# Four small moves in a two-layer attention kernel: context sums, context rows, the first pair's transposes, the gate products

## The chip, the core and the metric

One core of a Trainium2 chip. The time is the device time of one launch, in microseconds (us); a kernel's time is the median of its runs. The engines are named as the profile names them: PE (TensorE) does matmuls and transposes, DVE (VectorE), ACT (ScalarE) and POOL (GpSimd) work on rows, and SP (SyncE) issues most of the DMAs. ACT can issue DMAs too; an issue stands in ACT's queue like any instruction.

## The reference

Two adaLN-modulated blocks over 1024 latent tokens with a prefix of 256 context tokens, model width 1024, all in fp32. Layer 0 has grouped-query attention (16 heads of 64, 4 key heads), layer 1 latent attention (16 heads; keys and values from a compressed width of 256 and a shared rotary key of 32). Cut to one block:

```python
shift, scale, gate = split(silu(c) @ w_mod + b_mod, 3)
h = rms_norm(x, norm_w) * (1 + scale) + shift        # context: hc, with c_ctx
q, k, v, g = projections of h (and of hc)            # norms, rotary
o = softmax(q k^T * s) v      # latent queries: context and latent keys; context queries: context keys alone
x = x + gate * ((o * silu(g)) @ w_out)               # layer 0 does it for the context too
```

The output is the latent stream after both layers.

## The kernel before

Matmuls run on fp32r operands that are split into a high and a low part, so that a product is three matmuls: high by high (L120), low weight (L121), low activation (L122). The order on each engine is that of the code wherever a `manual_schedule` stands around it.

The program runs in stages, in this order: modulation and layer 0's projections; layer 0's attention; layer 0's output projection, which also makes the normed, modulated and transposed input of layer 1; layer 1's kv stage (compress, norm, expand to keys and values, tile by tile, as a software pipeline of stages written with `staged`); its q stage and gates; layer 1's attention; its output projection.

*Attention* (`Attention.run`) goes over units: a unit is a head group's or head's queries with its list `kts` of key tiles of 128. In layer 0 there are 20 units, 16 for latent queries ("lat", ten key tiles) and four for context queries ("ctx", two key tiles), the latter at positions 4, 9, 18 and 19. Layer 1 has 16 units of ten key tiles. For each unit the PE makes scores `st`, ACT the exponentials `p` of a tile of 128 x 1024 (L607), and the PE multiplies them with the values (L654, `av` or `avt`). Beside the scores of one unit the PE makes the maxima `mx` of a unit further on, which DVE reduces to `m` (L454, L486, L495, L497); the reduced maxima are turned (`turn` in `do_shift`, L95) and the rows written by DMA (L521) as `shift` or `shift_ctx`, which later scores subtract. The denominators are made in two ways. POOL adds a unit's `p` tiles into `acp` (`add_up`, L640); what it has not added is summed by DVE in blocks of 32 x 32 (`squares`, L99; then `total_by_squares`: four turns L95, two sums L705 and L706, the reciprocal L707), or else the PE sums `acp` by a matmul with a constant (`twos`, L720, then L724 and L725 on DVE). `total` chooses between the two by whether the unit has `squares`. SP then stores the reciprocals (`rrow`), reads them back spread over rows (`rb`) beside the SiLU gates (`sg`), POOL multiplies (L739, L740) and SP stores the result (`od`). In `run`, `n1` is how many of a unit's tiles POOL adds; `late` marks a context unit among the last two.

*The first output projection* (`out_proj(0, ...)`) goes over ten token tiles: `oraw` is loaded, split into `oh` (ACT) and `ol` (DVE), 48 matmuls make `y`, and DVE and POOL add gate times `y` to the residual `xt`. Its `sink0` stores the row, normalizes it (`norm_rows`) and, at every second tile, calls `flush`, which runs `modulate` for a pair of tiles: 16 PE transposes (L319) from the normalized `xt` (L307), then `hmod` on DVE, `hh` on ACT, `hl`. `hold` keeps pairs that are complete; a tile's sink is run before the next tile's matmuls are issued, so that `flush` at tile index 2 puts the transposes of pair 0 (tiles 0 and 1) between the matmuls of tile index 2 and those of tile index 3, the fourth.

*Layer 1's gate* is the product of `u` (the row silu(c)) with the third part of the modulation weights. It is made on DVE: for each of eight blocks `wcols` (512 KB) one `mod_cols` (L265), and at the end `mod_cols_end(2)`, which adds the bias (L271), turns (L95) and stores the row as `gated` (L274). The row is read back as `gb` when layer 1's output projection begins. In the kernel before this stands in the kv stage: the pipeline's third stage, `later_with_cols`, fetches and multiplies one block in each of the first eight tiles. `wcols` takes its buffers from `rawp` (`wraw`), from which the weights and the first `oraw` come too.

Of the kernel before, what the change touches and what calls it, by code (L numbers as in the profile page):

```python
# [10 lines left out]
F32 = mybir.dt.float32  # L11
# [8 lines left out]
P = 128  # L20
D = 1024
KT = D // P
# [4 lines left out]
TT = NT // P  # L27
# [5 lines left out]
def raw(ap):  # L33
    return ap.bitcast(F32)
# [3 lines left out]
def hybrid_kernel(ctx: ExitStack, tc: tile.TileContext, ins: dict, out: bass.AP):  # L38
# [31 lines left out]
    ud = dram.tile([2, D], F32, name="ud")  # L70
# [55 lines left out]
    def staged(items, *stages):  # L126

        items = list(items)
        held = {}
        for t in range(len(items) + len(stages) - 1):  # L130
            for j, stage in enumerate(stages):
                i = t - j
                if 0 <= i < len(items):
                    held[i] = stage(items[i], held.get(i))
# [127 lines left out]
    def mod_cols(w, u, junk, sec, k, conds):  # L262

        for j in conds:
            dve.scalar_tensor_tensor(junk, w, 0.5, u[:, j, :], op0=ALU.mult, op1=ALU.mult, accum_out=sums_of[sec][:, k, j:j + 1])  # L265
# [94 lines left out]
    class Attention:  # L360
        def __init__(self, l, units, ops):
            self.l, self.units, self.ops = l, units, ops
            self.state = {}
            self.vcache = {}
            self.kcache = {}
            self.sm = sm_pool
            self.step = 0
            self.deferred = []
            self.totals = []
            self.sums = 0  # L370
            self.running = False
            self.turns = []
            self.started = 0
            self.done = 0
            self.todo = []
            self.last_lat = [u for u in units if u["kind"] == "lat"][-1]

        def open_early(self, st):
# [131 lines left out]
        def do_shift(self, u):  # L510

            s = self.state[id(u)]
            m = tops[self.units.index(u) % 4]
            dve.reduce_max(m[:, :8], s["m"], axis=AX.X)

            def turn():
                at_ = (0, 32, 96)[self.units.index(u) % 3]
                r = turned[at_:at_ + 32, :]
                turn_squares(r, raw(m))
                for n in range(2):  # L520
                    (act if self.running else sp).dma_start(raw(s["crow"][n]), r[4 * n:4 * n + 4, :])  # L521

            self.turns.append((self.units.index(u), turn))

# [227 lines left out]
        def run(self, lead, ahead, extra, tail):  # L752
# [4 lines left out]
            with tc.manual_schedule(engines={mybir.EngineType.PE, mybir.EngineType.DVE, mybir.EngineType.Activation, mybir.EngineType.Pool}):  # L757
                for t, u in enumerate(self.units):
# [20 lines left out]
                    for group in (kts[:cut], kts[cut:]):  # L779
                        if not group:  # L780
                            continue
                        end = group[-1] == kts[-1]
                        final = t == len(self.units) - 1 and end
                        p2s = [self.pp.tile([P, 2, 1024], F32, name="p", tag="p", bufs=5) for _ in range(len(group) // 2)]
                        ps = [p2[:, a, :] for p2 in p2s for a in range(2)]

                        late = not whole and t >= len(self.units) - 2
                        n1 = len(ps) - (4 if end and (cut or final) else 2 if late or (whole and end) else 0)
                        for i, kt in enumerate(group):
                            self.run_deferred(self.step)  # L790
                            if HALVES[self.l]:
                                count += 1 if WIDE[self.l] else 2
                                self.scores_by_halves(u, kt, ps[i], self.next_maxima(count, t + 1 + ahead))
                            else:
                                self.do_scores(u, kt, ps[i], one_more)
                            self.step += 1
                            if i < n1:
                                self.add_up(u, [ps[i]], [])
                        if end and t + 2 < self.started:
                            self.state[id(self.units[t + 2])].pop("rest", lambda: None)()  # L800
                        if final:
                            tail()
                        if WIDE[self.l] and group[0] == kts[0]:
                            self.av_tile(u)
                        self.run_turns(next_turn)
                        if final:
                            self.add_up(u, [], ps[n1:])
                        if final:
                            self.run_deferred(self.step + 2)
                        gap = 0  # L810
                        while self.totals and (whole or late or final):
                            self.totals.pop(0)(gap, True)
                            gap += 3
                        if end and (whole or late) and not final:
                            if late:
                                self.add_up(u, [], [])
                            self.squares(u, p2s[n1 // 2:])
                        if t % 2 and end:
                            if parts:
                                parts()  # L820
                            parts = extra.pop(0)() if extra else None
                        self.do_av(u, group, ps)
                        self.step += (2 + len(group)) // 3
# [776 lines left out]
    with ExitStack() as st:  # L1600
# [16 lines left out]
        def sink0(tt, xt):  # L1617
            if tt < TL:
                sp.dma_start(x1d[tt * P:(tt + 1) * P, :], xt)
            norm_rows(xt, small)  # L1620
            xs_of.setdefault(tt // 2, []).append(xt)
            if tt % 2 == 0:
                flush(1)
            else:
                hold.append((tt // 2, xs_of[tt // 2]))

        def started0():
# [33 lines left out]
    with ExitStack() as st:  # L1661
# [96 lines left out]

        kept = []

        u = st.enter_context(tc.tile_pool(name="urow1", bufs=1, **right)).tile([P, D], F32, name="u0", tag="u0")
        sp.dma_start(u, ud[0:1, :].broadcast_to([P, D]))

        def gate_cols(k):
            w = rawp.tile([P, D], F32, name="wcols", tag="wraw")
            sp.dma_start(w, ins["l1_w_mod_t"][2 * D + k * P:2 * D + (k + 1) * P, :])
            mod_cols(w, u.unsqueeze(1), w, 2, k, (0,))
            if k == KT - 1:
                mod_cols_end(2)

        def store_all_but_last(tt, held):
            kept.append(held) if tt == TT - 1 else kv_store(tt, held)

        def later_with_cols(tt, kv):
            if tt < KT:
                gate_cols(tt)
            return kv

        with in_order(mybir.EngineType.DVE):
            staged(range(TT), kv_compress, kv_latent, later_with_cols, later, kv_expand, store_all_but_last)  # L1780
        wqa = load_weight(w_in1, KT, 288, 384)
        with tc.manual_schedule(engines={mybir.EngineType.PE, mybir.EngineType.DVE}):
            early[0] = proj1(0, wqa, 384)
# [234 lines left out]
    stL, stLP = ExitStack(), ExitStack()  # L2018
    at.open_late(stL, stLP)
    first = []  # L2020
    at.run(24, 2, pieces, lambda: first.extend(fetch_first(1, 3)))
    stLP.close()
    stE.close()
# [54 lines left out]
```

## Time and profile before

| | us |
|---|---|
| median of three runs | 1639.27 (1636.88 to 1641.38) |
| the profiled execution | 1638.23 |
| its span in the trace | 1636.3 |
| PE busy | 1596.0 |
| DVE busy | 1150.5 |
| POOL busy | 961.7 |
| ACT busy | 641.2 |

The profiled execution's own time is 1.93 us over its span. A row of the trace has the start, the duration, the engine, the line of the kernel, the operation, the tiles (out<-in), their shapes and a count where equal rows follow each other; in square brackets stands for how long the engine was idle before and what ended that. A matmul's row lasts longer than the distance to the next one, since matmuls overlap. "PEclk" is the clock that was granted to the PE, as a share of full speed.

### The profile page before, as it was taken

To read this page: it belongs to the slowest core of one execution; us is meant where nothing else is said; L and a number is where in the kernel's file an instruction comes from. 1 tells how busy PE (TensorE), PEld (TensorE's weight loads), DVE (VectorE), ACT (ScalarE), POOL (GpSimd) and SP (SyncE) were. 2 spreads that over 40 slices of the span, in tenths; PEclk is the share of its full clock that TensorE was granted. 3 is DMA by queue.
4 is the path that set the end of the run, shared out by engine and by line. 5 is a ranking of instruction groups with operands and counts; after the bars stand their busy time and mean duration, and the time that the engine had idled before them with its cause. 6 is when DMAs were issued, how large, how long until landed. Compare 5 with 4: busy or idle time off the path is not lost.

```text
span 1636.3 us, 26486 instructions
## 1 busy us (share of the span) xinstructions
PE 1596.0 (98%) x9788; PEld 1178.3 (72%) x9788; DVE 1150.5 (70%) x1951; ACT 641.2 (39%) x943; POOL 961.7 (59%) x629
## 2 busy tenths in 40 slices
PE   7999999999999999999989999999999999999998
PEld 5776788865554555577878798987776767767587
DVE  2674876679998988746576767755778888788231
ACT  3652321235654555522244543341444544435310
POOL 2673640138999999923245555450768878777521
PEclk9999999999999999999999999999999999999999
DMA  8636566742533342274246867768456565562451
GB/s 285 213 106 192 170 196 231 215 134 56 130 82 98 94 108 78 71 224 152 96 138 182 239 200 201 221 202 197 114 137 154 124 149 117 136 145 70 131 179 64
DMA packets 215325, 246.77 MB, mean 151 GB/s; under 512 B 19802, under 2 KB 157266, under 8 KB 215196
## 3 DMA queue, kind: packets, MB, share of 16 engines
q1 hardware_dynamic: 214228, 244.83, 53.7%
q8 instruction: 77, 1.26, 0.3%
q14 instruction: 52, 0.43, 0.1%
q10 hardware_dynamic: 968, 0.25, 0.1%
HBM read 171.23 MB, written 73.63 MB: 150 GB/s over the span
## 4 chain that ended last, share of the span: by engine, by line
PE 84%; DMA 5%; DVE 4%; POOL 2%; ACT 2%; issue 2%; SPq 1%; DVEq 0%; POOLq 0%; ACTq 0%
PE st L600 21%; PE avt L654 9%; PE av L654 9%; PE mm L120 8%; PE mm L122 8%; PE mm L121 8%; PE mx L452 4%; PE y L120 3%; PE y L121 3%; PE y L122 3%; PE mx L486 2%; DVE wb L163 1%; DMA q1l<-tl 1%; PE mx L462 1%; DMA mraw<-in_l_w_mod 1%
## 5 line engine op out<-in xcount | busy, mean ns | idle before, releaser
L640 POOL TENSOR_TENSOR acp<-acp,p 128x1024 f32<-128x1024 f32 x188 | 448.6, 2386 | 12.6
L607 ACT ACTIVATE p<-st 128x1024 f32<-128x1024 f32 x328 | 336.3, 1027 | 154.5 <-PE st L600 145.7
L454 DVE TENSOR_REDUCE m<-mx 128x1 f32<-128x512 f32 x256 | 175.8, 691 | 66.2 <-PE mx L452 60.3
L640 POOL TENSOR_TENSOR acp<-p 128x1024 f32<-128x1024 f32 x34 | 81.5, 2398 | 191.7 <-ACT p L607 191.7
L495 DVE TENSOR_REDUCE m<-mx 128x1 f32<-128x1024 f32 x128 | 150.2, 1219 | 39.4 <-PE mx L486 38.9
L654 PE MATMUL avt<-p,v 128*64 128x512 f32 x672 | 149.3, 596 | 0.7 <-ACT p L607 0.6
L654 PE MATMUL av<-p,v 128*64 128x512 f32 x640 | 141.1, 595 | 0.0
L163 POOL TENSOR_TENSOR wb<-wraw,wa 128x512 fp32r<-128x512 f32 (+3 forms) x65 | 91.0, 1415 | 80.4 <-ACT wa L184 80.4
L120 PE MATMUL mm<-wa,hh 128*128 128x512 f32 (+2 forms) x336 | 126.1, 375 | 1.7 <-ACT hh L1041 1.1
L600 PE MATMUL st<-QH,KH 64*128 64x512 f32 x320 | 122.5, 407 | 0.6 <-DVE gth L354 0.5
L122 PE MATMUL mm<-wa,hl 128*128 128x512 f32 (+2 forms) x336 | 121.5, 362 | 1.6 <-DVE hl L1044 1.6
L121 PE MATMUL mm<-wb,hh 128*128 128x512 f32 (+2 forms) x336 | 121.1, 360 | 0.0
L600 PE MATMUL st<-QH,KL 64*128 64x512 f32 x320 | 117.9, 391 | 0.0
L600 PE MATMUL st<-QL,KH 64*128 64x512 f32 x320 | 117.6, 390 | 0.0
L654 PEld LDWEIGHTS avt<-p,v 128*64 128x64 f32 x672 | 46.0, 137 | 93.8 <-issue 82.9
L654 PEld LDWEIGHTS av<-p,v 128*64 128x64 f32 x640 | 44.3, 137 | 87.9 <-issue 87.3
L120 PE MATMUL mm<-hh,wa 128*128 128x512 f32 (+1 forms) x264 | 103.0, 390 | 0.9 <-ACT th L102 0.9
L120 PE MATMUL y<-wa,oh 128*128 128x512 f32 (+1 forms) x268 | 103.3, 386 | 0.0
L122 PE MATMUL y<-wa,ol 128*128 128x512 f32 (+1 forms) x268 | 102.8, 384 | 0.0
L121 PE MATMUL y<-wb,oh 128*128 128x512 f32 (+1 forms) x268 | 102.8, 384 | 0.0
L122 PE MATMUL mm<-hh,wb 128*128 128x512 f32 (+1 forms) x264 | 101.3, 384 | 0.0
L121 PE MATMUL mm<-hl,wa 128*128 128x512 f32 (+1 forms) x264 | 101.3, 384 | 0.0
(267 smaller groups left out, 4045.1 us busy)
## 6 DMA issues: line engine op xcount, KB each, us to landing
wraw<-in_l_w_in SPq DMA_DIRECT2D x28, 512.0 KB
wcols<-in_l_w_mod_t SPq DMA_DIRECT2D x24, 512.0 KB
KH<-k1h SPq DMA_DIRECT2D x32, 320.0 KB
KL<-k1l SPq DMA_DIRECT2D x32, 320.0 KB
rb<-rrow SPq DMA_DIRECT2D x72, 128.0 KB
mraw<-in_l_w_mod SPq DMA_DIRECT2D x16, 512.0 KB
wraw<-in_l_w_out SPq DMA_DIRECT2D x16, 512.0 KB
QA<-q0h SPq DMA_DIRECT2D x32, 256.0 KB
```

The costliest lines, as they stand in the source:

```text
L120: pe.matmul(ps, lhsT=lh(k), rhs=rh(k), start=first and i == 0, stop=False)
L121: pe.matmul(ps, lhsT=lh(k), rhs=rl(k), start=False, stop=False)
L122: pe.matmul(ps, lhsT=ll(k), rhs=rh(k), start=False, stop=last and i == len(ks) - 1)
L163: eng.tensor_sub(lo, a, b)
L452: pe.matmul(held["m"][:, cs], lhsT=q[:, t * P:(t + 1) * P], rhs=k[:, ks], start=j == 0, stop=j == len(pairs) - 1)
L454: dve.reduce_max(s["m"][:, i, n:n + 1], held["m"], axis=AX.X)
L486: pe.matmul(m[:, n * 512:n * 512 + 512], lhsT=q[:, i * P:(i + 1) * P], rhs=k[:, n * 512:n * 512 + 512], start=True, stop=True)
L495: dve.reduce_max(s["m"][:, i, 0:1], m, axis=AX.X)
L600: pe.matmul(ps[:, n * 512:(n + 1) * 512], lhsT=lh, rhs=rh, start=j == 0, stop=j == last)
L607: act.activation(p, ps, AF.Exp, scale=self.ops["scale"])
L640: pool.tensor_add(t, a, b)
L654: pe.matmul(s["av"][64 * n:64 * n + 64, :], lhsT=s["v"][:, kt, u["vc"]:u["vc"] + 64], rhs=p[:, n * 512:(n + 1) * 512], start=kt == kts[0], ...
```

## The change

Four parts.

1. In `turn`, the rows of context units are issued by SP, in `run` as before it; those of latent units stay on ACT.
2. In `run`, every context unit now has all its `p` tiles summed by DVE's `squares`, not only the last two of them: POOL adds nothing for the units at positions 4 and 9, and the PE has no L720 for them.
3. In `sink0`, `flush` is not called at tile index 2 but at index 3, ahead of the transposes that follow at index 4 as before.
4. The eight `mod_cols`, their loads and `mod_cols_end(2)` leave the kv stage. A dictionary `beside` has them called in layer 1's attention, behind a unit's `squares`: loads of two blocks at unit 10, one product at each of units 11, 12 and 13, two at unit 14, and three with the end ahead of unit 15's first value products. Each product fetches the block after the next.

```diff
             self.todo = []
+            self.beside = {}
...
                 for n in range(2):
-                    (act if self.running else sp).dma_start(raw(s["crow"][n]), r[4 * n:4 * n + 4, :])
+                    (act if self.running and u["kind"] == "lat" else sp).dma_start(raw(s["crow"][n]), r[4 * n:4 * n + 4, :])
...
-                        n1 = len(ps) - (4 if end and (cut or final) else 2 if late or (whole and end) else 0)
+                        n1 = len(ps) - (4 if end and (cut or final) else 2 if end else 0)
...
-                        if end and (whole or late) and not final:
-                            if late:
+                        if end and not final:
+                            if not whole:
                                 self.add_up(u, [], [])
                             self.squares(u, p2s[n1 // 2:])
+                        self.beside.get((t, int(end)), lambda: None)()
...
-            if tt % 2 == 0:
+            if tt % 2 == 0 and tt != 2 or tt == 3:
                 flush(1)
-            else:
+            if tt % 2:
                 hold.append((tt // 2, xs_of[tt // 2]))
...
-        def gate_cols(k):
-            w = rawp.tile([P, D], F32, name="wcols", tag="wraw")
-            sp.dma_start(w, ins["l1_w_mod_t"][2 * D + k * P:2 * D + (k + 1) * P, :])
-            mod_cols(w, u.unsqueeze(1), w, 2, k, (0,))
-            if k == KT - 1:
-                mod_cols_end(2)
...
-            staged(range(TT), kv_compress, kv_latent, later_with_cols, later, kv_expand, store_all_but_last)
+            staged(range(TT), kv_compress, kv_latent, later, later, kv_expand, store_all_but_last)
...
+    def gate_fetch(k):
+        cols[k] = rawp.tile([P, D], F32, name="wcols", tag="wraw")
+        sp.dma_start(cols[k], ins["l1_w_mod_t"][2 * D + k * P:2 * D + (k + 1) * P, :])
+
+    def gate_cols(n):
+        for _ in range(n):
+            k = cols.pop("next", 0)
+            mod_cols(cols[k], u.unsqueeze(1), cols[k], 2, k, (0,))
+            cols["next"] = k + 1
+            if k + 2 < KT:
+                gate_fetch(k + 2)
+            if k == KT - 1:
+                mod_cols_end(2)
+
+    at.beside = {(10, 1): lambda: [gate_fetch(k) for k in range(2)], (11, 1): lambda: gate_cols(1), (12, 1): lambda: gate_cols(1),
+                 (13, 1): lambda: gate_cols(1), (14, 1): lambda: gate_cols(2), (15, 0): lambda: gate_cols(3)}
     at.run(24, 2, pieces, lambda: first.extend(fetch_first(1, 3)))
```

Line numbers of the changed kernel are one higher from L377 on, and two higher from about L818 on up to the kv stage.

What stands on the engines at three places follows. ACT's queue in layer 0's attention, before, at the start of the value products of the unit after the first context unit (`wa` is a cast of the next weights, `os` the copy of the last unit's result):

```order
L521 DMA shift<-turned 1x4x128 x2
L521 DMA shift_ctx<-turned 1x4x128 x2
L184 CAST wa<-wraw 128x512 x2
L675 COPY os<-avt 128x512
L607 ACTIVATE p<-st 128x1024 x10
```

The same place on ACT in the changed kernel, with the next unit's start:

```order
L522 DMA shift<-turned 1x4x128 x2
L184 CAST wa<-wraw 128x512 x2
L676 COPY os<-avt 128x512
L608 ACTIVATE p<-st 128x1024 x10
L522 DMA shift<-turned 1x4x128 x2
```

The two context rows are gone from ACT's queue; on SP they now stand between a load of `QA` and one of `QL`. DVE's queue in the first output projection, before, around the first pair's `hmod` (`yt` and `xt<-xt,yt` add a tile's result to its residual, `x_ms` and `xt<-xt,x_rs` normalize it):

```order
L307 TENSOR_SCALAR xt<-xt,x_rs 128x1024
L144 TENSOR_SCALAR x_ms<-xss 128x1
L888 TENSOR_TENSOR yt<-y,gb 128x512
L307 TENSOR_SCALAR xt<-xt,x_rs 128x1024
L888 TENSOR_TENSOR yt<-y,gb 128x512
L323 TENSOR_SCALAR hmod<-tp,A_114,B_116 128x256
L889 TENSOR_TENSOR xt<-xt,yt 128x512
L323 TENSOR_SCALAR hmod<-tp,A_114,B_116 128x256 x3
```

The same place in the changed kernel, from the second of those L307 on:

```order
L307 TENSOR_SCALAR xt<-xt,x_rs 128x1024
L890 TENSOR_TENSOR yt<-y,gb 128x512
L891 TENSOR_TENSOR xt<-xt,yt 128x512
L873 TENSOR_TENSOR ol<-oraw,oh 128x1024
L144 TENSOR_SCALAR x_ms<-xss 128x1
L307 TENSOR_SCALAR xt<-xt,x_rs 128x1024
L890 TENSOR_TENSOR yt<-y,gb 128x512 x2
L323 TENSOR_SCALAR hmod<-tp,A_114,B_116 128x256
```

One tile's work (add, split, norm) now lies between the second normalized row of the pair and the pair's first `hmod`; on the PE the fourth tile's 48 matmuls lie there. DVE's queue at the end of layer 1's attention, before, from unit 14's total on:

```order
L99 TENSOR_REDUCE squares<-acp 128x32
L95 STREAM_TRANSPOSE sums<-squares 32x96 x4
L705 TENSOR_REDUCE turned<-sums 32x32
L706 TENSOR_REDUCE turned<-turned 32x32
L707 RECIPROCAL turned<-turned 32x32
L871 TENSOR_TENSOR ol<-oraw,oh 128x896 x3
L724 STREAM_TRANSPOSE mx<-mx 128x256
```

The same place in the changed kernel, from unit 14's `squares` of its last two tiles on:

```order
L99 TENSOR_REDUCE squares<-p 128x64
L265 SCALAR_TENSOR_TENSOR wcols,cols_71<-wcols,u_11905 128x1024 x2
L99 TENSOR_REDUCE squares<-acp 128x32
L95 STREAM_TRANSPOSE sums<-squares 32x96 x4
L706 TENSOR_REDUCE turned<-sums 32x32
L707 TENSOR_REDUCE turned<-turned 32x32
L708 RECIPROCAL turned<-turned 32x32
L265 SCALAR_TENSOR_TENSOR wcols,cols_71<-wcols,u_11905 128x1024 x3
L271 TENSOR_TENSOR top_84<-cols_71,colsT 128x8
L95 STREAM_TRANSPOSE turned<-top_84 32x32 x4
L873 TENSOR_TENSOR ol<-oraw,oh 128x896 x3
```

Five of the eight products and the end stand in the last two units; the other three stand behind the `squares<-p` of units 11, 12 and 13, ahead of the maxima `m` of the unit after.

More of the change, by code (lines that the diff above doesn't have):

```diff
@@ L1759, in hybrid_kernel @@
         kept = []
-        u = st.enter_context(tc.tile_pool(name="urow1", bufs=1, **right)).tile([P, D], F32, name="u0", tag="u0")
-        sp.dma_start(u, ud[0:1, :].broadcast_to([P, D]))
-        def gate_cols(k):
-            w = rawp.tile([P, D], F32, name="wcols", tag="wraw")
-            sp.dma_start(w, ins["l1_w_mod_t"][2 * D + k * P:2 * D + (k + 1) * P, :])
-            mod_cols(w, u.unsqueeze(1), w, 2, k, (0,))
-            if k == KT - 1:
-                mod_cols_end(2)
         def store_all_but_last(tt, held):
             kept.append(held) if tt == TT - 1 else kv_store(tt, held)
[L1774 to L1777, printed above, removed]
         with in_order(mybir.EngineType.DVE):
-            staged(range(TT), kv_compress, kv_latent, later_with_cols, later, kv_expand, store_all_but_last)
+            staged(range(TT), kv_compress, kv_latent, later, later, kv_expand, store_all_but_last)
         wqa = load_weight(w_in1, KT, 288, 384)
@@ L2020, in hybrid_kernel @@
     first = []
+    u = stE.enter_context(tc.tile_pool(name="urow1", bufs=1, **right)).tile([P, D], F32, name="u0", tag="u0")
+    sp.dma_start(u, ud[0:1, :].broadcast_to([P, D]))
+    cols = {}
+    def gate_fetch(k):
[12 more added lines that the diff above has]
+                 (13, 1): lambda: gate_cols(1), (14, 1): lambda: gate_cols(2), (15, 0): lambda: gate_cols(3)}
     at.run(24, 2, pieces, lambda: first.extend(fetch_first(1, 3)))
```

## The prediction

> **What bounds the kernel now.** I read the page first (busy line, chain), then what the PE waited for, then 20 us windows for the places, and last the timelines of those places, engine by engine.
>
> ```profile
> PE 1596.0 (98%) x9788; PEld 1178.3 (72%) x9788; DVE 1150.5 (70%) x1951; ACT 641.2 (39%) x943; POOL 961.7 (59%) x629
> PE 84%; DMA 5%; DVE 4%; POOL 2%; ACT 2%; issue 2%; SPq 1%; DVEq 0%; POOLq 0%; ACTq 0%
> ```
> The PE works 1596.0 of 1636.3 us and carries 84% of the chain that ended last. So an edit is worth only what it takes from the PE's work or from its 40 us of idleness; time saved on another engine is worth nothing unless the PE waits there. The rows of the PE's waits (engine, line, waited-for; us, times, longest) that the change can touch:
>
> ```profile
> PE mmk L120 <- DVE kn L1714: 2.3, 2, 1.5
> PE tp L319 <- DVE xt L307: 2.2, 1, 2.2
> PE mx L486 <- DVE m L495: 1.9, 2, 1.4
> PE tp L1702 <- POOL kvn L1694: 1.4, 1, 1.4
> PE st L600 <- ACT os L675: 1.1, 1, 1.1
> PE mmv L120 <- ACT v L1736: 1.0, 1, 1.0
> ```
> They sum to 9.9 us: a ceiling for whatever only removes waits. The windows (length; PE, PEld, DVE, ACT, POOL busy; PE clock) show where the kv stage idles and where it doesn't, and one stretch at half clock:
>
> ```profile
> 742.00:744.00 2.00, 2.00 (x7) 1.71 (x6) 2.00 (x6) 1.90 (x5) 0.88 (x2) 0.51 0.22 53
> ...
> 840.00:860.00 20.00, 14.17 (x81) 10.82 (x80) 12.77 (x39) 8.95 (x28) 7.81 (x17) 1.00 0.46 151
> 880.00:900.00 20.00, 20.00 (x122) 17.88 (x122) 13.79 (x34) 9.26 (x25) 10.27 (x11) 1.00 0.76 210
> ```
>
> **Part 1, context rows on SP's queue.** In the attention unit that follows the first context unit (490 to 504 us):
>
> ```profile
> 491.09 5.32 ACTq L521 DMA_DIRECT2D shift<-turned  x2
> 496.98 2.38 ACTq L521 DMA_DIRECT2D shift_ctx<-turned  x2
> 499.40 1.14 ACT L184 CAST wa<-wraw 128x512 fp32r<-128x512 f32 x2 [8.68 <-DMA sg<-sgd]
> ...
> 495.85 2.31 DVE L99 TRANSPOSE_TENSOR_REDUCE squares<-p 128x64 f32<-128x2048 f32 x1
> 500.57 1.86 DVE L163 TENSOR_TENSOR wb<-wraw,wa 128x512 fp32r<-128x512 f32 x1 [2.41 <-ACT wa L184]
> ...
> 494.61 10.04 POOL L640 TENSOR_TENSOR acp<-acp,p 128x1024 f32<-128x1024 f32 x4
> ...
> 503.62 0.50 PE L486 MATMUL mx<-KA,QA 64*128 64x512 f32 x2 [1.35 <-DVE m L495]
> ```
> ACT issues two shift rows, done at 491.09 + 5.32 = 496.41, then two context rows until 499.36; only then come the weight casts, the copy `os` that the PE waits for, and DVE's `wb`, behind which the maxima `m` stand. Without the context rows the casts start near 496.45. The copy comes 2.9 us earlier and the PE's 1.1 for it is gone. `wb` can start behind DVE's own `squares`, which ends at 498.16, so 2.4 us earlier than 500.57, and the maxima with it: the PE's 1.35 is gone too. Ceiling 1.1 + 1.35 = 2.45. What may hold `wb` is POOL, whose four adds of 10.04 / 4 = 2.51 us run there and beside which it takes 1.86: one of them ends at 499.63, and if `wb` waits for it, only some 0.9 us are left of the move, and the gain is 1.1 + 0.5. Floor 0, if SP issues the rows so late that the context unit waits. I take **2.3**, near the ceiling, since both waits hang on the same ACT rows. The other context rows have no ACT work close behind: 0. On SP they stand between loads of Q that are issued two units ahead, so a late issue there meets slack: 0.
>
> **Part 2, sums of two context units by squares.** Removed, in each of two units: one POOL add, a group of PE matmuls and two short DVE rows. Added on DVE: one `squares<-p` of 2.31 (row above) and a total as the last units already have it.
>
> ```profile
> 447.41 0.64 PE L720 MATMUL mx<-acp,twos 128*32 128x256 f32 x8
> ...
> 435.95 4.79 DVE L495 TENSOR_REDUCE m<-mx 128x1 f32<-128x1024 f32 x4 [2.31 <-PE mx L486]
> ...
> 526.73 1.96 DVE L163 TENSOR_TENSOR wb<-wraw,wa 128x512 fp32r<-128x512 f32 x1 [1.76 <-ACT wa L184]
> ...
> 700.57 0.97 DVE L95 STREAM_TRANSPOSE sums<-squares 32x64 f32<-32x64 f32 x4
> ...
> 702.44 0.34 DVE L707 RECIPROCAL turned<-turned 32x32 f32<-32x32 f32 x1
> ```
> PE: 0.64 a group, twice, is 1.28 at most. DVE: 2.31 + (702.78 - 700.57 = 2.21) = 4.5 us more per unit. What hides it: the `squares` falls into DVE's idle 2.31 before 435.95 and 1.76 before 526.73; it overruns them by up to 0.55 us (2.31 - 1.76), and then the PE waits for `m`. The total falls behind a unit's last maxima, under the PE's value products of that unit. If that cover went, up to 2.21 per unit would land on the PE. Bounds +1.28 and 1.28 - 2 x 2.21 = -3.1; I take 1.28 - 0.55 = **0.7**, by the idle rows, which are those of the very place.
>
> **Part 3, first pair behind tile four.**
>
> ```profile
> 736.66 0.39 PE L122 MATMUL y<-wa,ol 128*128 128x512 f32 x1
> 737.34 0.30 PE L319 MATMUL tp<-ident,xt 128*128 128x128 f32 x1 [0.29 <-DVE x_ms L144]
> 739.80 2.81 PE L319 MATMUL tp<-ident,xt 128*128 128x128 f32 x15 [2.16 <-DVE xt L307]
> 742.26 0.78 PE L120 MATMUL y<-wa,oh 128*128 128x512 f32 x1
> ...
> 764.68 0.40 PE L122 MATMUL y<-wa,ol 128*128 128x512 f32 x1
> 766.58 0.48 PE L120 MATMUL y<-wa,oh 128*128 128x512 f32 x1
> ...
> 729.41 1.23 DVE L871 TENSOR_TENSOR ol<-oraw,oh 128x1024 fp32r<-128x1024 f32 x1 [1.99 <-ACT oh L870]
> ```
> From a tile's last matmul to the next tile's first it takes 742.26 - 736.66 = 5.60 us at the first pair and 766.58 - 764.68 = 1.90 at the second. Now tile four's 48 matmuls (its operand `ol` was ready at 730.64) stand in that gap: two tiles take 764.68 - 742.26 = 22.4 us, so 11 us cover a normalized row that came 0.29 + 2.16 = 2.45 us late. That gives 3.70, and some 0.7 more as the first matmuls behind the gap run in the window of clock 0.51: **4.4**. [...] Bounds 2.45 (the waits alone) and 4.5 (all of it). Late next: the residuals' loads for tiles five and six, which wait for the moved transposes, 11 - 3.7 = 7 us later; they are needed at a tile's end, so 0.
>
> **Part 4, gate products.** In the kv stage:
>
> ```profile
> 850.56 1.41 POOL L1694 TENSOR_TENSOR kvn<-krt,krt 128x32 f32<-128x32 f32 x1
> 854.22 0.25 POOL L1694 TENSOR_TENSOR kvn<-krt,krt 128x32 f32<-128x32 f32 x1
> ...
> 850.65 1.20 DVE L265 SCALAR_TENSOR_TENSOR wcols<-wcols,u 128x1024 f32<-128x1024 f32 x1
> 907.53 1.84 DVE L265 SCALAR_TENSOR_TENSOR wcols<-wcols,u 128x1024 f32<-128x1024 f32 x1
> 909.96 0.86 DVE L95 STREAM_TRANSPOSE turned<-top 32x32 f32<-32x32 f32 x4
> ```
> The small POOL row takes 0.25 alone and 1.41 beside the product, and the PE waits 1.4 for it: 1.41 - 0.25 = 1.2 gained. At the stage's end the last product and its turn hold DVE for 1.84 + 0.86 = 2.7 us ahead of the sums from which `kn` comes; the PE's waits on `kn` and `v` there are 2.3 + 1.0 = 3.3, so the 2.7 comes off them in full. Between, the window 880 to 900 has a PE busy 20.00 of 20: 0. The stage's SP queue loses eight loads of 512 KB, and the next weights' loads come forward into their buffers; as no PE wait there is on a load, that is 0 as well. Gain **3.9**, bounds 1.2 (only the POOL row) and 5.
>
> Their new place costs. Eight products (1.2 to 1.84 each, as above), one turn, eight loads of 512 KB and one store are now in the last units of layer 1's attention:
>
> ```profile
> 1394.94 1.39 DVE L454 TENSOR_REDUCE m<-mx 128x1 f32<-128x512 f32 x2 [2.03 <-PE mx L452]
> ...
> 1540.35 3.77 DVE L871 TENSOR_TENSOR ol<-oraw,oh 128x896 fp32r<-128x896 f32 x3 [16.54 <-ACT oh L870]
> ...
> 1538.54 1.28 POOL L739 TENSOR_TENSOR rb<-rb,sg 128x512 f32<-128x512 f32 x1
> ...
> 1541.94 0.64 PE L720 MATMUL mx<-acp,twos 128*32 128x256 f32 x8
> ...
> 1532.04 1.75 SPq L839 DMA_DIRECT2D oraw<-od  x3
> ```
> Three stand each ahead of a unit's first maxima, where DVE idles 2.03: hidden with 0.2 to 0.8 to spare. Five stand in the last two units, where DVE idles 16.54. What they delay there: POOL's last adds, by up to 5 x 0.6 = 3 us, which now end at 1538.54, just in time for the PE's 1541.94 (3.4 us of slack); and on SP the store of the gates waits for the last three products and the turn, 3 x 1.84 + 0.86 = 6.4 us of DVE, with `sg`, `od` and `oraw` queued behind it, so `oraw` leaves up to 6 us later than 1532.04; its `ol` rows begin only at 1540.35, so 8 us cover that. Bounds 0 and 4 (both covers short by 2); I take **0.35** lost, by the POOL slack, which nearly closes. The loads themselves meet attention's open DMA: 0.
>
> **Sum.** 2.3 + 0.7 + 4.4 + 3.9 - 0.35 = 10.95. The profiled execution took 1638.23 (span 1636.3 and 1.93 around it), 1.04 below the median of 1639.27. By it the new run is 1627.3, by the median 1628.3; I say **1628**. What a measurement can't tell from no change is 0.3%, 4.9 us.
>
> **Rivals.**
> *A. The kv stage's gain stays out.* For it: the waits at its end are named `kn` and `v`, whose own chain runs over POOL and ACT. Against: the product's row stands right inside. Gain 1.2 instead of 3.9: 1631.
> *B. DVE becomes the bound around the context units.* It is given 4.5 us in each of two units; if half falls on the PE, part 2 is 1.28 - 4.5 = -3.2, and if part 1's `wb` comes late again too: 10.95 - 3.9 - 2.3 = 4.75, so 1628 + 6.2 = 1634.2. Against: the idle rows above.
> *C. The tail.* `oraw` or POOL late by 3 us more: 1631.
> *D. Slower.* One mechanism: a product and a POOL add stretch each other (1.41 for 0.25 and 1.84 for 1.20 above). [...] If each of the eight products waits out one add (2.51) and then runs its 1.84 before the maxima, it holds DVE 4.35, 2.3 over the idle 2.03; the PE loses 8 x 2.3 = 18.6: 1628 + 18.6 = 1647. It turns the sign from 1.4 us per product on. Against: only three of the eight stand ahead of maxima, and DVE idles 16.54 at the others.
> *E. The pair's wait only moves* to the second pair, which keeps its place: the gain of part 3 falls to 0, 1632.4. Against: the second pair had no wait.
>
> **How the numbers follow.** The forecast 0.56 (own range 1624 to 1632: parts 1 and 3 at their floors or ceilings); A 0.12, C 0.10, E 0.04, all still faster; B 0.12, two thirds of it within 0.3% of 1639.3; D 0.06. Faster: 0.56 + 0.12 + 0.10 + 0.04 - 0.07 for runs that scatter (1636.88 to 1641.38) + 0.04 = 0.79; the same 0.15; slower 0.06. The range 1622 to 1637 holds the forecast, A, C, E and most of B.
>
> **What would show it.** Right: no waits of the PE on `os` L676 and `m` L496 near 500, on `xt` L307 and none at half clock near 740, on `kvn` and `kn` near 852 and 915; two L721 groups fewer; 1480 to 1540 as full as before. Wrong: PE waits on `m` after 435, on `m` L455 near 1345 to 1420, or on `oh`, `ol` or `acp` near 1542.

## The result, and the profile after

The changed kernel takes 1622.83 us (median of five, 1619.86 to 1629.01), the kernel before 1638.89 in the same comparison (five, 1636.88 to 1641.38). The ratio is 0.9907, 95% interval 0.9883 to 0.9932: about 15 us faster. That is 5 us below the forecast of 1628: inside the stated range of 1622 to 1637, but by 0.8 us only, and outside the 1624 to 1632 that the forecast had for itself.

The page of the changed kernel, with its span, the busy line and the chain by engine:

```profile
span 1621.0 us, 26450 instructions
PE 1590.0 (98%) x9772; PEld 1183.6 (73%) x9772; DVE 1163.5 (72%) x1963; ACT 641.7 (40%) x943; POOL 956.0 (59%) x627
PE 83%; DVE 8%; DMA 2%; POOL 2%; issue 2%; ACT 2%; SPq 1%; ACTq 0%; DVEq 0%; POOLq 0%
```

The PE is still the bound: of the 15.3 us that the span lost, 6.0 are PE work or PE time at half clock (1596.0 to 1590.0) and 9.3 are idleness. What the PE waits for now, in the rows that answer to those of before:

```profile
PE tp L1703 <- DVE kvn L1684: 3.7, 3, 1.3
PE mx L487 <- DVE m L496: 2.5, 3, 1.2
...
PE y L108 <- ACT oh L872: 1.3, 2, 0.7
...
PE mmk L120 <- DVE kvn L1685: 0.7, 1, 0.7
...
PE tp L1704 <- POOL kvn L1696: 0.4, 2, 0.2
PE mmv L120 <- ACT v L1738: 0.3, 1, 0.3
```

The waits on `xt` L307, on the copy `os` and on `kn` are gone, and those on POOL's `kvn` and on `v` are small. The first row was 3.7 before as well. Two rows went up: the maxima `m` (1.9 to 2.5) and `oh` (0.6 to 1.3; the second of its waits, at the start of the last output projection, is new).

To see where time went, take one PE instruction in both records and subtract its start times; the change of that difference over a stage is what the stage gained or lost. The table does so against the first record of the kernel before (negative is faster; us). "Start" is up to 433 us, "attention 0" from there to its last value products, "output 0" to the kv stage's first transposes, "kv" to its last, "q, gates" to attention 1's first value products, "attention 1" to its last, "end" to the first matmul of the last output projection. Behind that the records agree within 0.6.

| record | start | attention 0 | output 0 | kv | q, gates | attention 1 | end |
|---|---|---|---|---|---|---|---|
| changed kernel | -2.57 | -1.23 | -4.55 | -7.83 | -1.12 | +1.16 | +0.81 |
| changed kernel, again | -2.69 | -1.40 | -4.55 | -7.82 | -1.37 | +1.13 | +1.56 |
| kernel before, again | -2.74 | -0.20 | +2.05 | +1.42 | -1.57 | +1.44 | 0 |
| part 1 alone | -3.30 | -1.42 | +2.41 | +1.40 | -2.92 | +0.61 | 0 |
| part 2 alone | -1.97 | -2.52 | -1.43 | +2.63 | +0.52 | +0.16 | 0 |
| part 3 alone | -3.44 | -0.32 | -3.90 | +0.03 | -0.45 | +0.55 | 0 |
| part 4 alone | -2.55 | -0.43 | +2.43 | -7.81 | -1.95 | -0.17 | +1.15 |
| changed, without part 2 | -2.06 | -1.40 | -4.55 | -7.31 | -3.42 | +1.13 | +0.93 |
| before, products in mid kv stage | -3.81 | -0.33 | +1.24 | -2.06 | -3.57 | +1.25 | 0 |
| parts 1 to 3, products in mid kv stage | -4.19 | -1.80 | -4.55 | -2.17 | -3.24 | +1.44 | 0 |
| changed, gate store by ACT | -3.43 | -1.40 | -4.56 | -7.91 | -1.82 | +1.12 | 0 |
| changed, split products | -1.14 | -1.31 | -4.55 | -7.75 | -3.13 | -0.03 | 0 |

The changed kernel's row sums to -15.33; the spans differ by 15.3. The kernel before's second row shows how far a column moves from one execution to the next of the same program: up to 2.7. The growth of 1.1 to 1.4 that some rows have in attention 1 is called the drift below. The changed kernel's start column is not the change's: no instruction ahead of 433 us was changed, and every other record starts ahead of the first one of before, the kernel before's second record too.

### The profile page after: what moved, and what is told of

It is laid out like the page before. It is cut to its first block, busy times and chain, and to the rows that moved or that the text cites. A ratio compares the mean times of both kernels' runs of the same rounds, so it can differ in the third digit from the quotient of the medians.

```text
span 1621.0 us, 26450 instructions
## 1 busy us (share of the span) xinstructions
PE 1590.0 (98%) x9772; PEld 1183.6 (73%) x9772; DVE 1163.5 (72%) x1963; ACT 641.7 (40%) x943; POOL 956.0 (59%) x627
## 4 chain that ended last, share of the span: by engine, by line
PE 83%; DVE 8%; DMA 2%; POOL 2%; issue 2%; ACT 2%; SPq 1%; ACTq 0%; DVEq 0%; POOLq 0%
PE st L601 19%; PE mm L120 8%; PE avt L655 8%; PE mm L122 8%; PE mm L121 8%; PE av L655 8%; PE mx L453 4%; PE y L122 4%; PE y L121 4%; PE y L120 4%; PE mx L487 2%; DVE wb L163 1%; DMA q1l<-tl 1%; DVE squares L99 1%; DVE m L496 1%
## 5 line engine op out<-in xcount | busy, mean ns | idle before, releaser
L641 POOL TENSOR_TENSOR acp<-p 128x1024 f32<-128x1024 f32 x32 | 76.8, 2401 | 196.0 <-ACT p L608 190.2
```

Of the source, the lines that this page charges most:

```text
L641: pool.tensor_add(t, a, b)
```

## The experiments

**Each part alone.** The edits are the four pieces of the diff above, each applied by itself to the kernel before.

> Part 1 alone (context rows issued by SP). The prediction's working: 2.3 us, all of it at the unit after the first context unit (before's 489.61 to 513.31, 23.70 us, becomes 21.4). Theory from the changed kernel's trace: its PE is 1.9 us further ahead over that unit, 0 elsewhere, so 1.9. Rival: the 1.9 needed part 2 as well (POOL's missing add lets the weight row go earlier), then this alone gives under 1. A second theory rides along: the first 2.6 us of the changed kernel's lead are there before any changed instruction (at 34 us) and come from a stretch of half clock near 27 to 34 us that only some executions have; then this kernel's lead at 400 us is anything between 0 and 3 us, by whether its record shows that stretch.

Measured: 1635.24 us against 1637.77, ratio 0.9983 (0.9974 to 0.9993). Attention 0 gained 1.42. ACT, DVE and POOL in that record, at the place that the prediction quoted:

```profile
488.09 3.70 ACTq L521 DMA_DIRECT2D shift<-turned  x2
491.83 1.14 ACT L184 CAST wa<-wraw 128x512 fp32r<-128x512 f32 x2 [4.15 <-DVE sums L95]
495.45 0.59 ACT L675 COPY os<-avt 128x512 f32<-128x512 f32 x1 [2.48 <-PE avt L654]
...
495.09 2.71 DVE L163 TENSOR_TENSOR wb<-wraw,wa 128x512 fp32r<-128x512 f32 x1
...
494.86 2.40 POOL L640 TENSOR_TENSOR acp<-acp,p 128x1024 f32<-128x1024 f32 x1
```

The casts follow the shift rows at once, `wb` follows DVE's squares without a gap, and the copy `os` waits for the PE instead of the other way round. But `wb` itself now takes 2.71 instead of 1.86, and a wait on `m` of 1.1 remains. What sets the end of `wb` is POOL's add: 494.86 + 2.40 = 497.26, and `wb` ends at 497.80, 0.54 later. In all 13 records `wb` at this place ends 0.54 or 0.55 after the add beside which it starts, and with no POOL row beside it a `wb` of DVE took 0.65 (part 2 alone, at 523.99). The add ends 9.9 after POOL's row `rb` has started, and the PE's maxima `mx` start 11.6 after that same start, in every record. So this stall ends by POOL's `rb`, not by ACT's casts. The rival (under 1) falls; the theory's 1.9 and the prediction's 2.3 were both too much.

> Part 2 alone (sums of the context units at positions 4 and 9 by squares). The prediction's working: 0.7 us gained. Theory from the changed kernel's trace: each unit gains 0.55 (the matmul group) and gives back 0.6 (the PE waits for the maxima behind the new squares), so 0.0, within 0.3; the PE's wait on m L495 grows by about 1.2. Rival: DVE's 4.5 us more per unit reach the PE, 2 to 4 us lost.

Measured: 1635.61 us, ratio 0.9991 (0.9981 to 1.0002). Attention 0 gained 2.52, which neither theory had. Step by step along the PE: 0.55 and 0.56 for the two missing matmul groups, 0.6 given back after unit 4, and some 2.1 gained at 500 us, the stall that part 1 removes too, although the context rows are still on ACT here:

```profile
489.29 3.12 ACTq L521 DMA_DIRECT2D shift<-turned  x2
493.04 2.63 ACTq L521 DMA_DIRECT2D shift_ctx<-turned  x2
495.71 1.14 ACT L184 CAST wa<-wraw 128x512 fp32r<-128x512 f32 x2 [6.79 <-DMA shift_ctx<-turned]
```

The two shift rows take 3.12 us to issue and not 5.32. POOL's row `rb`, on which the stall hangs, in the kernel before and in part 1 alone:

```profile
492.03 1.28 POOL L739 TENSOR_TENSOR rb<-rb,sg 128x512 f32<-128x512 f32 x1 [2.09 <-DMA rb<-rrow]
```

```profile
487.38 1.27 POOL L739 TENSOR_TENSOR rb<-rb,sg 128x512 f32<-128x512 f32 x1 [0.82 <-DMA rb<-rrow]
```

In the five records without part 1 and part 2 it waits 1.8 to 2.1 us for its DMA, in the eight with either of them 0.4 to 0.9; so that goes with the program and not with the execution. Counted from one instruction ahead of the place, `rb` starts 1.35 earlier in part 1 alone and 1.98 in part 2 alone, and the PE's `mx` 1.33 and 1.96. SP issues the DMA at the same time within 0.8 in all of them. What makes it land earlier with either part is open, and so is, with it, by what path part 1 gains.

> Part 3 alone (first pair behind tile four). The prediction's working and the trace agree: 4.4 to 4.6 us, between the third tile's matmuls and the end of the next tile; no half-clock stretch near 740. Rival: by idle time alone 2.45. The rest of the program moves along unchanged: the lead at 1540 us equals that at 760 us within 0.5.

Measured: 1632.24 us, ratio 0.9962 (0.9947 to 0.9977). Output 0 gained 3.90, there is no half clock near 740, and the lead at 1540 us (7.53) is that at 840 (7.66). That is a little under the 4.4 to 4.6 expected, while the time's gain, 5.5 us in the median, is above it; the half clock of the kernel before, taken up below, differs from one execution to the next.

> Part 4 alone (gate products at the end of layer 1's attention). The prediction's working: 3.9 gained in the kv stage, 0.35 lost at the attention's end: 3.5. Theory from the changed kernel's trace: 7.6 gained in the kv stage, since the products of the first tiles stand in the serial chain of the pipeline's start (three tiles at 1.2 us each) besides the 3.7 at the end; 0.8 lost between the last value products and the first output matmul; a drift of up to 1.2 us over the attention's units that has nothing to do with the products. Sum 5.5 to 7. Rival: the kv stage's 7.6 came from the other parts' earlier arrival (other DMA neighbours), then 4 here.

Measured: 1627.86 us, ratio 0.9936 (0.9921 to 0.9951). The kv stage gained 7.81 with no other part of the change in the program, so the rival falls; the end lost 1.15; attention 1 did not drift. The time's gain of 9.9 us is beyond the 5.5 to 7 expected. Part of that is the clock: of the five records whose first tiles hold products, three have a stretch at half clock near 850, and their kv columns are 1.4 to 2.6 above that of the first record, which has none; no record without such products has it. So the part takes some 7.8 us off the stage where that stretch is missing and 9.2 to 10.4 where it falls. The kv stage's gain has two places. DVE at the start of that stage's pipeline, where each tile's statistics `kvms` wait for the tile before. Before:

```profile
848.21 0.13 DVE L1678 TENSOR_SCALAR kvms<-kvss 128x1 f32<-128x1 f32 x1
...
851.86 0.13 DVE L1678 TENSOR_SCALAR kvms<-kvss 128x1 f32<-128x1 f32 x1
...
855.98 0.13 DVE L1678 TENSOR_SCALAR kvms<-kvss 128x1 f32<-128x1 f32 x1
```

And the same rows in the changed kernel:

```profile
839.84 0.13 DVE L1680 TENSOR_SCALAR kvms<-kvss 128x1 f32<-128x1 f32 x1
...
842.34 0.13 DVE L1680 TENSOR_SCALAR kvms<-kvss 128x1 f32<-128x1 f32 x1
...
844.86 0.13 DVE L1680 TENSOR_SCALAR kvms<-kvss 128x1 f32<-128x1 f32 x1
```

A tile took 3.65 and 4.12 us, now 2.50 and 2.52: the product (1.20 and its read of 0.07) stood in a serial chain over DVE, POOL, ACT and PE, and the PE had nothing else to do yet. The PE's waits of before show it too; these three rows, all from 853 to 864, are gone in the changed kernel:

```profile
PE mmv L120 <- ACT sq L1729: 0.8, 1, 0.8
PE mmk L120 <- ACT v L1736: 0.7, 1, 0.7
PE mm L120 <- ACT v L1736: 0.7, 1, 0.7
```

Along the PE's own stream that start gives 3.5 us up to 866 us of the first record and 3.8 up to 873, and the stage's last tiles, from 909 on, another 3.8.

**The second part of the stall near 500 us: part 2 taken out.**

```diff
-                        n1 = len(ps) - (4 if end and (cut or final) else 2 if end else 0)
+                        n1 = len(ps) - (4 if end and (cut or final) else 2 if late or (whole and end) else 0)
...
-                        if end and not final:
-                            if not whole:
+                        if end and (whole or late) and not final:
+                            if late:
```

> The changed kernel without part 2. The first experiments showed part 1 alone gaining 1.4 us and part 2 alone 2.6 us over the same units, both together 1.7: they share one stall (near 500 us), and neither adds to the other. Theory: without part 2 the changed kernel's lead over the units from 430 to 560 us is 1.4, against 1.7 with it, so a time within 1 us of the changed kernel. Rival, the prediction's working: 0.7 worse. Rival by part 2 alone: 2.6 worse.

Measured: 1622.58 us, ratio to the kernel before 0.9901 (0.9881 to 0.9920), against the changed kernel's 0.9907 in another comparison. Attention 0's column is -1.40, with part 2 it is -1.23 and -1.40. Part 2 adds nothing beside part 1. (The kernel with parts 1 to 3 and the products in the middle of the kv stage has -1.80 there, so this is good to 0.4.) Where its matmuls' 1.1 us go, on the PE of the kernel before and then twice on that of the changed kernel:

```profile
529.88 0.50 PE L486 MATMUL mx<-KA,QA 64*128 64x512 f32 x2 [0.57 <-DVE m L495]
```

```profile
456.67 0.50 PE L487 MATMUL mx<-KA,QA 64*128 64x512 f32 x2 [0.46 <-DVE m L496]
...
526.17 0.50 PE L487 MATMUL mx<-KA,QA 64*128 64x512 f32 x2 [1.25 <-DVE m L496]
```

The first wait of the changed kernel is new, the second stood at 0.57. On DVE ahead of the second of them:

```profile
521.34 2.31 DVE L99 TRANSPOSE_TENSOR_REDUCE squares<-p 128x64 f32<-128x2048 f32 x1 [0.74 <-ACT p L608]
523.57 1.41 DVE L163 TENSOR_TENSOR wb<-wraw,wa 128x512 fp32r<-128x512 f32 x1
524.91 4.60 DVE L496 TENSOR_REDUCE m<-mx 128x1 f32<-128x1024 f32 x4
```

The squares wait 0.74 for the exponentials before they run their 2.31, so they don't fill DVE's idle time from its start, and `wb` and the maxima come behind. `wb` takes 1.41 here, beside a POOL row `rb` that runs from 523.14 to 524.44; in part 2 alone that row comes later, `wb` takes 0.65, and the PE waits 0.49.

**Products in the middle of the kv stage**, on the kernel before and together with parts 1 to 3.

```diff
-            if tt < KT:
-                gate_cols(tt)
+            if 3 <= tt < 7:
+                gate_cols(2 * tt - 6)
+                gate_cols(2 * tt - 5)
```

> The kernel before, with the gate products still in the kv stage but two each in its tiles 3 to 6 instead of one each in tiles 0 to 7; no other part of the change. Theory: only the products in the start of the pipeline (tiles 0 to 2, a serial chain over DVE) and the last one cost; in the middle the PE has work in store. Then the kv stage gains 6 to 7.9 us, as much as with the products out of it, and nothing is lost later. Rival: a product costs its 1.2 us wherever it stands on DVE in that stage, or two in a row are more than the middle can cover: gain under 3 or a loss.

> Parts 1, 2 and 3 as in the changed kernel, and the gate products two each in tiles 3 to 6 of the kv stage instead of at the attention's end. If the middle of the kv stage covers them, this has the changed kernel's gain without its loss of 0.8 to 1.2 us at the attention's end: 0 to 1.2 us faster than the changed kernel. If not, 1 to 5 us slower than it.

Measured: 1633.73 us (0.9964; 0.9951 to 0.9977) and 1626.65 us (0.9928; 0.9910 to 0.9945). The theory was half right, and the kv column's 2.1 is the rival's "gain under 3". The pipeline's start gains its 3.5 and the end about 3.3, but the middle loses 4.8, so 2.1 remain. The PE's waits in the first of the two over the kv stage:

```profile
PE tp L1701 <- DVE kvn L1682: 3.7, 3, 1.3
PE mmv L120 <- DVE kvn L1683: 3.4, 3, 1.7
PE mmv L120 <- ACT v L1736: 1.3, 1, 1.3
```

The second row is new, and the third stood at 1.0: two products in a row, 2.5 us, are more than the middle covers. With the end free of products the second kernel loses nothing between attention 1 and the output projection, and its median is still 3.8 us above the changed kernel's, from another comparison and with overlapping intervals.

**The gate's store on ACT.** In the changed kernel SP's queue reads, at attention 1's end:

```profile
1518.80 0.30 SPq L274 DMA_DIRECT2D gated<-turned  x1
1519.19 0.45 SPq L735 DMA_DIRECT2D sg<-sgd  x1
1519.73 1.19 SPq L745 DMA_DIRECT2D od<-os  x2
...
1522.88 1.86 SPq L841 DMA_DIRECT2D oraw<-od  x3
```

The store of the gates comes first, behind DVE's products and turn:

```profile
1502.15 3.37 DVE L265 SCALAR_TENSOR_TENSOR wcols<-wcols,u 128x1024 f32<-128x1024 f32 x1
...
1511.13 2.29 DVE L265 SCALAR_TENSOR_TENSOR wcols<-wcols,u 128x1024 f32<-128x1024 f32 x1
...
1513.35 2.28 DVE L265 SCALAR_TENSOR_TENSOR wcols<-wcols,u 128x1024 f32<-128x1024 f32 x1
...
1515.67 2.20 DVE L271 TENSOR_TENSOR top<-cols,colsT 128x8 f32<-128x8 f32 x1
```

and what waits for it in the end is the PE:

```profile
1528.91 0.50 PE L108 MATMUL y<-wa,oh 128*128 128x512 f32 x1 [0.74 <-ACT oh L872]
```

The edit puts the end of the products behind the first loads of `oraw` and issues the store from ACT, which is idle there:

```diff
-            if k == KT - 1:
-                mod_cols_end(2)
...
-            sp.dma_start(gated[1][0:1, :].rearrange("o (k p) -> (o k) p", p=P), r[:KT, :])
+            act.dma_start(gated[1][0:1, :].rearrange("o (k p) -> (o k) p", p=P), r[:KT, :])
...
+    def fetch_then_store():
+        first.extend(fetch_first(1, 3))
+        mod_cols_end(2)
...
-    at.run(24, 2, pieces, lambda: first.extend(fetch_first(1, 3)))
+    at.run(24, 2, pieces, fetch_then_store)
```

> The changed kernel, but the end of the gate products is put behind the first loads of the output projection in the program, and its store is issued by ACT, so that SP's queue no longer waits for it ahead of the loads oraw. Theory: the 0.8 to 1.2 us lost between the last value products and the first output matmul are that wait; oraw leaves SP some 5 us earlier (at 1517 to 1518 on the changed kernel's clock instead of 1522.9), the PE's wait on oh goes, 0.8 us gained. Rival: the loss is POOL's, which is stretched by the products; then nothing is gained.

Measured: 1619.96 us, ratio to the kernel before 0.9886 (0.9866 to 0.9905). SP and PE at the same place:

```profile
1515.90 1.73 SPq L841 DMA_DIRECT2D oraw<-od  x3
...
1526.24 0.50 PE L108 MATMUL y<-wa,oh 128*128 128x512 f32 x1
```

This kernel is 1.85 us further ahead by then; on the changed kernel's clock `oraw` leaves at 1517.8, 5 us earlier, as expected. The first output matmul follows without a wait: the end column is 0. That the loss was SP's queue is shown: the eight products stand at the same units beside POOL's adds as in the changed kernel, where POOL's `rb` takes 2.27 at 1510.07 against 1.28 before, and the end column is 0 all the same. The edit moves the store behind the loads and to another queue at once, so which of the two would do alone is not shown.

**One product a tile, and none in the last unit.**

```diff
+            if 3 <= tt < 7:
+                k = tt - 3
+                w = rawp.tile([P, D], F32, name="wcols", tag="wraw")
...
-    at.beside = {(10, 1): lambda: [gate_fetch(k) for k in range(2)], (11, 1): lambda: gate_cols(1), (12, 1): lambda: gate_cols(1),
-                 (13, 1): lambda: gate_cols(1), (14, 1): lambda: gate_cols(2), (15, 0): lambda: gate_cols(3)}
+    at.beside = {(10, 1): lambda: [gate_fetch(k) for k in (4, 5)], (11, 1): lambda: gate_cols(1), (12, 1): lambda: gate_cols(1),
+                 (13, 1): lambda: gate_cols(1), (14, 1): lambda: gate_cols(1)}
```

> The changed kernel with the gate's store on ACT, and the products split: one each in tiles 3 to 6 of the kv stage, one each at units 11 to 14 of layer 1's attention, none in unit 15. Theory: the middle of the kv stage covers one product a tile (the kernel before showed a busy PE there) but not two, which cost 4.7 us; so the kv stage keeps its 7.9 us and the attention's end has 1.2 to 3.4 us less of stretched rows; within 1 us of the kernel with the store on ACT alone. Rival: a product costs 0.6 us in the middle too, 2.4 us worse.

Measured: 1619.33 us, ratio 0.9900 (0.9883 to 0.9917). The kv column is -7.75, the end 0: one product a tile in the middle is covered, two are not. With the store on ACT it makes no difference whether the last unit holds products. The medians of these two kernels lie 3 us below the changed kernel's, but in other comparisons, in which the kernel before differs by up to 3.5 us; the ratios are 0.9886 and 0.9900 against 0.9907, with overlapping intervals. That they are faster than the changed kernel is shown at the end column alone.

**Second records.**

> The kernel before, unchanged, for a second record of it. Theory: the first record's 6.83 us at half clock near 27 us, in none of the changed kernels' records, is a matter of the single execution, so this record is 2 to 4 us ahead at 350 us; near 740, where the PE idles, half clock shows again (four of five records with that gap had it). Rival: the early stretch belongs to the program, and this record starts like the first.

> The changed kernel, unchanged, for a second record of it. Theory: layer 1's attention units last 25.47 us instead of 25.29 in every second unit, as in its first record, since that goes with the program and not with the execution; no half clock near 740. Rival: the units' length is a matter of the execution, and this record has the kernel before's alternation of 25.29 and 25.43.

Measured: one time each, 1638.66 and 1623.04. The window from 26 to 34 us in the first and in the second record of the kernel before (PE busy in 8 us, then PEld, DVE, ACT, POOL, and the granted clock):

```profile
26.00:34.00 8.00, 7.38 (x24) 5.85 (x24) 3.48 (x8) 4.29 (x8) 2.51 (x2) 0.57 0.75 244
```

```profile
26.00:34.00 8.00, 7.38 (x57) 5.50 (x61) 4.90 (x10) 4.20 (x8) 2.53 (x2) 1.00 0.84 274
```

The same program did 24 matmuls in one execution and 57 in the other. So the start's 2.6 us are the execution's. The second theory fell: the kernel before's second record has the longer attention units (attention 1 +1.44, where its first record sets the 0), so the drift goes with the execution as well. Both records of the changed kernel have it.

## Why the prediction was right or wrong

*Part 1, 2.3 predicted: 1.4.* The place and the two waits were right, the releaser was not. The prediction named POOL's add as what may hold `wb`, with a gain of 1.6, and set that aside because both waits hang on the same ACT rows. In every record `wb` ends 0.54 or 0.55 behind that add, so the earlier casts bring the maxima nothing, and the 1.3 to 1.4 that came is that POOL's `rb` starts 1.35 earlier, which the prediction did not see.

*Part 2, 0.7 predicted: 0 beside part 1, within 0.2.* The 1.28 of matmuls were 1.1; the overrun, taken as 0.55 in the unit with the shorter idle time, is a new wait of 0.46 in one unit and a wait of 1.25 instead of 0.57 in the other, 1.1 together. The squares must wait for the exponentials (0.74), and I let them start where DVE's idle time starts; in the second unit `wb` then meets a POOL row as well. That parts 1 and 2 share a stall was not seen: the sum treated them as independent.

*Part 3, 4.4 predicted: 4.55,* with both terms, the gap and the slow matmuls behind it. The clock's share depends on the execution, though, so that the two agree this closely is luck of the record that was read. Output 0 without part 3 stands at 0, +2.05, +2.41, -1.43, +2.43 and +1.24 in six records, with 3.4, 6.8, 6.8, 0, 6.8 and 3.4 us at half clock near 740; with part 3 it is -3.9 to -4.56 in seven, with none. So the part is worth 3 us in an execution without that stretch and up to 7 in one with a long one, which is above the prediction's upper bound. The bounds of 2.45 and 4.5 came from one record. The profile's windows at the place, in the second record of the kernel before and in the changed kernel:

```profile
740.00:744.00 4.00, 4.00 (x14) 3.38 (x13) 4.00 (x8) 2.73 (x5) 2.65 (x3) 0.54 0.40 106
```

```profile
740.00:744.00 4.00, 4.00 (x20) 3.25 (x19) 1.35 (x2) 0.06 (x1) 0.74 (x1) 1.00 0.49 136
```

*Part 4's gain, 3.9 predicted with bounds 1.2 and 5: 7.8.* This is the largest miss, and the step is named in the prediction: "the PE waits 1.4 for it: 1.41 - 0.25 = 1.2 gained" counted one POOL row as all that the products cost in the stage's first tiles. The window from 840 to 860 with a PE busy 14.17 of 20 was quoted and not followed further. That stretch is a pipeline filling, in which a DVE row costs its whole length: 3.5 to 3.8 us for three products. At the end 3.8 came off, where I took 2.7: the waits on `kn` and `v` there were 3.3, and the rest stands in no wait row. In the middle the 0 was right for one product a tile.

*Part 4's cost, 0.35 predicted: 0.8 to 1.6.* The mechanism was named (the store at SP's head, `oraw` behind it, up to 6 us late; measured 7), and the cost lies between the 0.35 and the 3 us more of rival C. Mis-sized was the cover of 8 us. I read it from the start of `ol`, which ACT's exponentials had held up; `oh` could then run at 1523 at once, and the delayed load ended later than that. POOL's slack, by which I set the 0.35, had no part in it.

*Of the rivals,* D's stretched rows are there: the eight products, seven of them 1.20 or 1.21 long before and one 1.84, take 1.33 to 3.37 beside POOL's rows, and an addition of 128 x 8, 0.15 before, takes 2.20. The 128 x 8 row ends at 1517.87, at the end of a POOL add (1517.85), `wb` 0.54 or 0.55 behind its add, and in the changed kernel's first record each of the eight products 1.08 or 1.09 behind the POOL row beside which it starts. D's 4.35 for each product, a whole add and then 1.84, was an estimate that no run shows: the longest took 3.37, and 3.38 in part 4 alone. But most of the stretching falls where DVE has nothing else to do: the three products ahead of maxima take 1.33 to 1.47, within the idle 2.03, and attention 1's column in part 4 alone is -0.17. A and E did not happen; of B there are the waits of 0.46 and 1.25, not 4.5.

*The sum.* Predicted 10.95. From the changed kernel's first record: 1.23 + 4.55 + 7.83 - 0.81 = 12.8 for what the parts did, 2.57 for the start and 1.12 for the q stage and gates, which I did not trace further (that column is about 2 us lower in the records without a half-clock stretch near 1000), less 1.16 of the drift. Parts 1 and 2 fell short by 1.8 and part 4 went beyond by 3.5. So the time came inside the range partly by luck: the misses have opposite signs, and the start's 2.57, which helped, has nothing to do with the change. In the medians the four parts alone gained 2.5, 2.2, 5.5 and 9.9 us, 20 together, against 16 for the whole change; the stall that parts 1 and 2 share accounts for some 2.6 of the difference, and the rest is within the scatter.

## What to carry to other kernels

Work on an engine that is idle on average can still cost its full length where a pipeline fills or drains, as the three products at the start of the kv stage did (3.5 to 3.8 us for three of 1.2); look at the stretches in which the bound engine's window is not full, and move such work to one where it is. When work moves, follow every queue that it enters: here the DMA at the head of SP's queue cost 0.81 to 1.56 us at the end, and the eight operations on DVE cost 0 there once the store was on ACT. And two edits near one stall are not added: each may remove the same wait (here 1.42 and 2.52 alone, 1.23 and 1.40 together). Where a row ends at a fixed distance behind a row of another engine in every record, as `wb` does here with 0.54 or 0.55, look for its releaser there, even if the view names another.

## What the runs showed of the hardware

The half-clock stretches, with a granted clock of 0.50, last 3.41 or 6.83 us in the records, apart from one at each record's very end, and lie where the PE has just idled: in the first records of the two kernels they start within 0.73 us of the end of an idle time of 0.62 (near 27), 2.16 (near 740) and 2.03 and 2.01 us (near 1000). They are not in every execution: near 740 in five of the six records with a gap there and in none of the seven without; near 850 in three of the five with products in the first tiles, near 1000 in five of all. Near 740 the PE waited 2.45 us in two pieces, 0.29 and 2.16, with a transpose between. Ahead of the stretch near 850 in the second record of the kernel before it idled 1.19, 1.36 and 0.68 us, with matmuls between:

```profile
853.00:856.00 3.00, 2.98 (x9) 2.23 (x10) 1.55 (x5) 0.64 (x5) 1.19 (x4) 0.50 0.52 183
```

Its first record has waits of 1.19, 1.37 and 0.68 us at the same place, and a granted clock of 1.00 from 840 to 860. What decides whether the clock halves behind such waits is open. For a kernel that idles as briefly as this one, at most 2.16 us at a time between matmuls in that record, one record tells the wait but not the clock that follows.

A second thing is open. In layer 1's attention two streams of matmuls with 64 rows each run side by side. In the first record of the kernel before they start in pairs:

```profile
1297.68 0.40 PE L452 MATMUL mx<-KH,QH 64*128 64x512 f32 x1
1297.68 0.40 PE L600 MATMUL st<-QH,KH 64*128 64x512 f32 x1
...
1299.29 0.40 PE L452 MATMUL mx<-KH,QH 64*128 64x512 f32 x1
```

In its second record they are 0.08 to 0.1 us apart there, and a key tile takes 1.62 us instead of 1.61:

```profile
1296.93 0.40 PE L600 MATMUL st<-QH,KH 64*128 64x512 f32 x1
1297.01 0.40 PE L452 MATMUL mx<-KH,QH 64*128 64x512 f32 x1
...
1298.55 0.40 PE L600 MATMUL st<-QH,KH 64*128 64x512 f32 x1
1298.65 0.40 PE L452 MATMUL mx<-KH,QH 64*128 64x512 f32 x1
```

The stage has 16 units of ten key tiles, so 0.01 us a tile is about the size of the drift of 1.1 to 1.4 us. What sets the streams apart in one execution and not in the other was not tried.
